# The last products of a hybrid decoder block: two pieces of 256 tokens, and final norms with tokens on partitions

## The chip, the cores and the metric

The kernel runs on one core of one Trainium2 chip. The core has TensorE (PE, matrix products into PSUM banks of 128 partitions by 512 fp32 columns), VectorE (DVE), ScalarE (ACT), GpSimd (POOL) and SyncE (SP, which issues the transfers here). The metric is the device time of one launch in microseconds, the median of several runs. The program before takes 983.76 us (three runs, 981.42 to 987.34).

## The reference

One decoder block on x of 1024 tokens by 1024 features in fp32, with shift, scale and gate columns made from a vector c:

```python
    for i in range(DEPTH):
        cond = c_act @ ada_w[i] + ada_b[i]
        shift1, scale1, gate1, shift2, scale2, gate2 = jnp.split(cond, N_MOD, axis=-1)
        h = modulate(rmsnorm(x, norm1_g[i]), shift1, scale1)
        ...
        x = x + gate1[:, None, :] * (y @ w_out[i])

        h2 = modulate(rmsnorm(x, norm2_g[i]), shift2, scale2)
        g_ff, up_ff = jnp.split(h2 @ w_ffn_in[i], 2, axis=-1)
        x = x + gate2[:, None, :] * ((jax.nn.silu(g_ff) * up_ff) @ w_ffn_out[i])

    shift_f, scale_f = jnp.split(c_act @ ada_f_w + ada_f_b, 2, axis=-1)
    return modulate(rmsnorm(x, norm_f_g), shift_f, scale_f)
```

What matters here is the end: the product with `w_ffn_out`, its addition to x, and the final norm over the 1024 features of each token, with its scale and shift.

## The kernel before

Everything is held with features on partitions: x is sixteen tiles of 128 features by 512 tokens, eight (k = 0 to 7) for each half of the tokens (half 0: tokens 0 to 511, half 1: 512 to 1023). Matmuls take fp32 operands split into a high and a low part, and three matmuls stand for one product of a 128x128 weight tile.

The feed-forward's second product is computed by a scheme of seven products in place of eight (Strassen-Winograd, on the two halves of the tokens and the two halves of features), in three rounds over the inner dimension (`ROUNDS`: 4, 4 and 3 pairs of tiles). For each n of 0 to 3 there are seven products m, each over the round's pairs; in the last round one product is 3 pairs x 3 matmuls = nine matmuls of 512 columns. `step(n, m)` (L1408) runs one: products 1, 6, 7, 4 add up in a bank B, 5 and 3 in a bank C, 2 in a bank A, and after each product DVE adds the bank's present state, times the gate, to one x tile (L1419). `DESTS` says to which: 1, 2 and 4 go to half 0, and 5, 7, 6 and 3 to half 1; 2 and 3 finish the tile k = n of their half, 4 and 5 finish k = n + 4. So half 0 is done with (3, 4), half 1 with the last of the C products. `begin_out(n)` loads and splits the weights of n; with `KEPT` those of products 5 and 3 for n = 1 to 3 lie in buffers that nothing else needs then.

In the last round the list at L1442 gives the order: behind half 0's last product (3, 4) come (1, 3), (2, 3), (3, 5) and (3, 3), of which only (3, 3) is cut into two pieces of 256 tokens. `pieces` (L1327) are half 0, and the first and second 256 tokens of half 1; each has a final norm of its own.

The final norm: `square` (L1339) squares a finished x tile on ACT (L1343). Early squares are added up on POOL (L1348) into `sums`; late ones go straight to `to_partitions` (L1330), which sums over the 128 features on PE: `ones` spread to 32 columns is the stationary side, 128 tokens of the square are the moving side, and the four groups of tokens land on four groups of 32 partitions (L1335). `early_sums` (L1354) does so for the POOL sums. `norm(i)` (L1359) takes the root on ACT (L1364), the reciprocal on DVE (L1365; both on tiles with 128 columns) and spreads the result over all partitions by matmuls (L1367) with a picking column `sel_tok` as the stationary side. `output(i)` (L1370) multiplies x with scale and norm on DVE (L1385), or on POOL (L1382) from a copy (L1376), adds the shift on ACT (L1387, L1383) and stores rows of 512 columns (L1389).

The order of each engine is not that of the text. `fix_order` (L493) takes all instructions, gives each a duration (`duration`, L131; `Clock.tensor`, L338, adds a price when PE changes between matmuls that use only part of its rows or columns and whole ones), and runs a list scheduler several times over the whole program with ranks from its own backward run; the best order found is laid down for each engine, SP's transfers with it. `issue_after` holds PE instructions behind a given one. Each engine then runs its queue in order.

Of the kernel before, what the change touches and what calls it, by code (L numbers as in the profile page):

```python
# [7 lines left out]
F32 = mybir.dt.float32  # L8
F32R = mybir.dt.float32r
BF16 = mybir.dt.bfloat16  # L10
AF = mybir.ActivationFunctionType
ALU = mybir.AluOpType
# [21 lines left out]
N_FILL = 8  # L34
N_POOL_TAPS = (6, 6)
IDLE = (0, 3, 3)
DIAGONAL = ('n2_0', 'a1', 'b1', 'n2_1', 'g10', 'g11')

SHIFT1, SCALE1, GATE1, SHIFT2, SCALE2, GATE2, SHIFTF, SCALEF = range(8)
# [91 lines left out]
def duration(s):  # L131

    width = max([o.width for o in s.reads + s.writes] or [0])
    two_in = sum(o.space == "SB" for o in s.reads) >= 2
    if s.engine == "PE":
        n, m = s.writes[0].width, s.reads[1].width
        if not s.reads[0].f32:
            t = n / 512 * 0.2267
        else:
            k = s.reads[0].box[1] - s.reads[0].box[0]  # L140
            t = {128: 0.219, 32: 0.068}.get(m, 0.109 if k > 64 else 0.055) * n / 128
        return t, t + 0.176, 0
    if s.engine == "Activation":
        psum = any(o.space == "PSUM" for o in s.reads)
        t = 0.238 + width * 0.0007 if psum else 0.2 + width * 0.00085
        t += 0.08 * sum(o.width == 1 for o in s.reads[1:])
        return (t + 0.1, t + 0.105, 0) if len(s.writes) > 1 else (t - 0.097, t + 0.009, 0)
    if s.engine == "DVE":
        if s.kind in ("Memset", "BNStatsAggregate"):
            return 0.09, 0.18, 0  # L150
        if s.kind == "BNStats":
            return 0.61, 0.7, 0
        if s.kind == "Reciprocal":
            t = 0.95 if width >= 128 else 0.17
# [174 lines left out]
class Clock:  # L329
# [7 lines left out]

    def tensor(self, t, s):  # L338

        if s.partial != self.partial:  # L340
            self.partial = s.partial
            t += 0.09 if s.partial else 0.12
        w = int(t / CLOCK_WINDOW)
        slow = 2 if self.throttled and self.active.get(w - 1, 0.0) < CLOCK_WINDOW / 2 else 1
        end = t + slow * s.issue
        a = t
        while a < end:
            w = int(a / CLOCK_WINDOW + 1e-9)
# [161 lines left out]
def block_kernel(ctx: ExitStack, tc: tile.TileContext, xT, c, ada, cols, vbias, bs, wsp,  # L510
# [88 lines left out]
    def load_late():  # L599
        t = front.tile([P, 2 * H], F32R, tag="wt", name="late")  # L600
        late.update(diag=t[:, 0:H], low=t[:, H:H + P], picks=t[:, H + P:H + P + 2 * P + 1])
        raw = tmp("picks_raw")[:, 0:2 * P + 1]
        nc.sync.dma_start(raw, cst[:, P + 34:])
        A.activation(late["picks"], raw, AF.Copy)
        G.memset(late["diag"].bitcast(F32), 0.0)

# [717 lines left out]
            nc.sync.dma_start(xs[half][i], x_mid[half][i])  # L1324


    pieces = [slice(0, H), slice(H, H + 256), slice(H + 256, S)]  # L1327
    sums, squares_in, norm_banks = {}, [0, 0, 0], {}

    def to_partitions(i, t):  # L1330

        part = pieces[i]
        nq = (part.stop - part.start) // P
        for q in range(nq):
            PE.matmul(norm_banks[i][q * 32:(q + 1) * 32, 0:P], ones.broadcast_to([P, 32]),  # L1335
                      t[:, q * P:(q + 1) * P], start=squares_in[i] == 0, stop=False, skip_group_check=True)
        squares_in[i] += 1

    def square(k, half, cols=None, late=False):  # L1339

        part = cols or (slice(0, H) if half == 0 else slice(H, S))
        t = ev(f"sq_nf{half}_{k}_{part.start}")[:, 0:part.stop - part.start]
        A.activation(t, x_tile(k, part), AF.Square)  # L1343
        if not late:
            if half not in sums:
                sums[half] = t
            else:
                G.tensor_tensor(sums[half], sums[half], t, op=ALU.add)  # L1348
            return
        for i, p in enumerate(pieces):  # L1350
            if p.start >= part.start and p.stop <= part.stop:
                to_partitions(i, t[:, p.start - part.start:p.stop - part.start])

    def early_sums(half):  # L1354
        for i, p in enumerate(pieces):
            if (p.start >= H) == (half == 1):
                to_partitions(i, sums[half][:, p.start - half * H:p.stop - half * H])

    def norm(i):  # L1359
        bank, part = norm_banks[i], pieces[i]  # L1360
        nq = (part.stop - part.start) // P
        rows = slice(0, nq * 32)
        rt = sb.tile([P, P], F32, tag="rt", name=f"rt_nf{i}", bufs=2)[rows]
        A.activation(rt, bank[rows, 0:P], AF.Sqrt, bias=epst[rows], scale=1.0 / D)  # L1364
        V.reciprocal(rt, rt)  # L1365
        for q in range(nq):
            PE.matmul(bank[:, q * P:(q + 1) * P], sel_tok[rows, q:q + 1].broadcast_to([nq * 32, P]),  # L1367
                      rt, start=True, stop=True)

    def output(i, tiles=range(KD), by_pool=()):  # L1370
        bank, part = norm_banks[i], pieces[i]
# [3 lines left out]
            r = ev(f"r_nf{i}")[:, 0:size]  # L1375
            A.activation(r, bank[:, 0:size], AF.Copy)  # L1376
        for k in tiles:
            if k % per_store == 0:
                row = ev(f"of{i}_{k}")
            t = row[:, k % per_store * size:(k % per_store + 1) * size]  # L1380
            if k in by_pool:
                G.tensor_tensor(t, x_tile(k, part), r, op=ALU.mult)  # L1382
                A.activation(t, t, AF.Identity, bias=ccol(SHIFTF, k), scale=ccol(SCALEF, k))  # L1383
            else:
                V.scalar_tensor_tensor(t, x_tile(k, part), ccol(SCALEF, k), bank[:, 0:size],  # L1385
                                       op0=ALU.mult, op1=ALU.mult)
                A.activation(t, t, AF.Identity, bias=ccol(SHIFTF, k))  # L1387
            if (k + 1) % per_store == 0:
                nc.sync.dma_start(out[(0, KD, KD + KD // 2)[i] + k // per_store], row)  # L1389
# [4 lines left out]
    for r, pairs in enumerate(ROUNDS):  # L1394
# [13 lines left out]
        def step(n, m, cols=slice(0, H)):  # L1408
# [1 line left out]
            if m == 1:  # L1410
                b_banks[n] = mm_bank(f"B{r}_{n}")
            if m == 5:
                c_banks[n] = cv_bank(f"C{r}_{n}")
            bank = c_banks[n] if m in (5, 3) else gn_bank(f"A{r}_{n}") if m == 2 else b_banks[n]
            ins = product(bank, st[n][m], [v[m] for v in mov], m in (1, 5, 2), cols)
            k, half = DESTS[m]
# [23 lines left out]
            continue  # L1440
        begin_out(0)
        for n, m in ((0, 1), (0, 5), (0, 6), (0, 2), (0, 7), (1, 1), (0, 4), (0, 3), (1, 6), (1, 2), (1, 7),  # L1442
                     (2, 1), (1, 4), (2, 2), (2, 6), (3, 1), (2, 7), (3, 2), (3, 6), (2, 4), (1, 5), (3, 7),
                     (2, 5), (3, 4)):
            if m == 1 and n:
                begin_out(n)
            last_ins = step(n, m)
            if m in (2, 4):
                if n == m == 2:
                    norm_banks[0] = nrm_bank("ssq_nf0")  # L1450
                square(n if m == 2 else n + 4, 0, late=n == 3)
            elif (n, m) in ((0, 7), (1, 5), (2, 5)):
                square(n + 4, 1)
            elif (n, m) == (0, 3):
                square(0, 1)
            if (n, m) == (3, 7):
                early_sums(0)


    with issue_after(last_ins):  # L1460
        step(1, 3)
        square(1, 1)
        norm(0)
        step(2, 3)
        norm_banks[1], norm_banks[2] = gn_bank("ssq_nf1"), mm_bank("ssq_nf2")
        square(2, 1, late=True)
        early_sums(1)
        step(3, 5)
        square(7, 1, late=True)
        output(0, (0, 1, 2, 4), by_pool=())  # L1470
        for part in pieces[1:]:
            step(3, 3, slice(part.start - H, part.stop - H))
            square(3, 1, part, late=True)
    with tc.high_priority():
        norm(1)
        norm(2)
    output(0, (3, 5, 6, 7), by_pool=(3, 5))
    output(1)
    output(2)

# [82 lines left out]
```

## Time and profile before

| | |
|---|---|
| runs | 983.76 us median (981.42, 983.76, 987.34) |
| profiled execution | 983.2 us, of which its span is 981.5 us |
| PE busy | 956.0 us, 97% of the span |
| DVE busy | 873.5 us, 89% |
| mean granted clock of TensorE | 0.994 |
| transfers | 142.18 MB read, 41.16 MB written |

The span is cut into 40 slices on the page; a digit is the busy share in tenths:

```profile
PE   7999999999999999999999999999999999999994
DVE  6989999989999762899999999999778989869936
ACT  6777467543473752564332233333337437236416
POOL 0068888656464312665444444455442200000121
PEclk9999999999999999999999999999999999999997
```

In a row of the timeline or of a group stand the engine, the line, the operation, the tile written and the tiles read, and the count; "x8" behind a line of four matmuls says that each fp32 matmul is two instructions. A matmul's duration contains its way through the array, so that the distance between starts is shorter than the duration of one. The chain of waits goes back from the program's end and names at each step what released the next. A table by stretches gives for each stretch the busy time of each engine with its count of instructions, the granted clock, the share of the transfer engines that was busy, and GB/s.

### The profile page before, as it was taken

The numbers are of one execution on the slowest core, as the hardware profiler recorded it, in microseconds if no ns is written. First come the engines' busy times: TensorE is split into PE (matmuls) and PEld (weight loads), VectorE is DVE, ScalarE is ACT, GpSimd is POOL, SyncE is SP. The second block draws the span as 40 slices with busy tenths as digits, with TensorE's granted clock in tenths as the row PEclk, the third lists the DMA queues.
The fourth block names the chain that finished last, engine by engine and source line by source line (L and its number), as shares of the span: only waits on it lengthen the run. The fifth ranks groups of instructions, "written<-read, shape, count | busy, mean of one in ns | idle before, by whom it ended". The sixth has DMA issues, their size and how long they took to land.

```text
span 981.5 us, 13035 instructions
## 1 busy us (share of the span) xinstructions
PE 956.0 (97%) x4563; PEld 769.1 (78%) x4563; DVE 873.5 (89%) x1232; ACT 475.1 (48%) x755; POOL 403.6 (41%) x233
## 2 busy tenths in 40 slices
PE   7999999999999999999999999999999999999994
PEld 4877777778777778788888878888887888888873
DVE  6989999989999762899999999999778989869936
ACT  6777467543473752564332233333337437236416
POOL 0068888656464312665444444455442200000121
PEclk9999999999999999999999999999999999999997
DMA  9982442434476434744677776867657848315104
GB/s 341 334 317 69 164 158 64 143 122 150 144 249 192 145 133 160 264 174 150 214 242 238 240 247 232 260 226 252 202 185 263 285 155 261 112 56 159 33 1 172
DMA packets 70355, 184.19 MB, mean 188 GB/s; under 512 B 7825, under 2 KB 8209, under 8 KB 70290
## 3 DMA queue, kind: packets, MB, share of 16 engines
q1 hardware_dynamic: 70290, 183.37, 55.8%
q8 instruction: 36, 0.59, 0.3%
q14 instruction: 29, 0.24, 0.1%
HBM read 142.18 MB, written 41.16 MB: 187 GB/s over the span
## 4 chain that ended last, share of the span: by engine, by line
PE 76%; DVE 17%; ACT 2%; issue 2%; DMA 2%; POOL 1%; SPq 0%; ACTq 0%; DVEq 0%; POOLq 0%
PE B L1065 27%; PE C L1065 16%; PE ah L1065 9%; DVE cv L998 6%; PE po L675 3%; PE po L677 3%; PE po L676 3%; PE p L675 3%; PE A L1065 3%; PE p L676 3%; PE p L677 3%; DVE w_f L1058 1%; DVE ada L629 1%; DVE t_h L687 1%; PE pm L939 1%
## 5 line engine op out<-in xcount | busy, mean ns | idle before, releaser
L1065 PE MATMUL B<-h,w_f 128*128 128x512 f32 x816 | 190.3, 390 | 1.3 <-DVE x L1285 0.9
L1065 PEld LDWEIGHTS B<-h,w_f 128*128 128x128 f32 x816 | 152.8, 188 | 34.7 <-DVE x L1285 1.7
L998 DVE SCALAR_TENSOR_TENSOR cv<-ypad,colt,cv 128x512 f32<-128x512 f32 x216 | 146.6, 746 | 0.1
L1065 PE MATMUL B<-fa,w_d 128*128 128x512 f32 x528 | 125.7, 390 | 0.3 <-DVE x L1419 0.3
L1065 PE MATMUL C<-h,w_f 128*128 128x512 f32 x528 | 123.4, 389 | 0.0
L1065 PEld LDWEIGHTS B<-fa,w_d 128*128 128x128 f32 x528 | 98.7, 188 | 22.0 <-DVE x L1419 0.8
L1065 PEld LDWEIGHTS C<-h,w_f 128*128 128x128 f32 x528 | 99.1, 188 | 20.6
L1065 PE MATMUL ah<-h,wh_a 128*128 128x512 f32 x320 | 101.8, 395 | 1.1 <-DVE ahead L1082 0.7
L1057 ACT ACTIVATE w_d<-raw_d 128x512 fp32r<-128x512 f32 (+1 forms) x72 | 42.1, 594 | 84.1 <-PE B L1065 33.0
L1348 POOL TENSOR_TENSOR sq_nf<-sq_nf,sq_nf 128x512 f32<-128x512 f32 x9 | 12.5, 1389 | 170.5 <-ACT sq_nf L1343 170.5
L659 POOL TENSOR_TENSOR wl_a<-raw_a,wh_a 128x1024 fp32r<-128x1024 f32 x20 | 49.6, 2481 | 78.0 <-ACT wh_a L658 78.0
L1308 POOL TENSOR_TENSOR x<-x,up 128x512 f32<-128x512 f32 x20 | 34.8, 1741 | 101.6 <-ACT x L1307 101.6
L1057 ACT ACTIVATE w_f<-raw_f 128x512 fp32r<-128x512 f32 x68 | 42.4, 627 | 67.6 <-PE B L1065 37.3
L1065 PEld LDWEIGHTS ah<-h,wh_a 128*128 128x128 f32 x320 | 59.8, 188 | 16.3 <-issue 1.2
L1058 DVE TENSOR_TENSOR w_f<-raw_f,w_f 128x512 fp32r<-128x512 f32 x68 | 70.4, 1040 | 2.4 <-ACT w_f L1057 2.2
L1065 PE MATMUL C<-fa,w_d 128*128 128x512 f32 (+1 forms) x273 | 64.4, 384 | 0.0
L1065 PE MATMUL ah<-h,wl_a 128*128 128x512 f32 x160 | 62.7, 393 | 0.0
L1065 PEld LDWEIGHTS C<-fa,w_d 128*128 128x128 f32 x273 | 50.0, 188 | 10.8 <-issue 1.0
L1058 DVE TENSOR_TENSOR fa<-a,fa 128x512 fp32r<-128x512 f32 x77 | 52.4, 721 | 1.3 <-ACT fa L1057 1.2
L1419 DVE SCALAR_TENSOR_TENSOR x<-B,cond,x 128x512 f32<-128x512 f32 x48 | 35.6, 744 | 18.8 <-PE B L1065 18.6
L1057 ACT ACTIVATE fa<-a 128x512 fp32r<-128x512 f32 x77 | 46.4, 626 | 6.0 <-DMA a<-acts 2.9
L1058 DVE TENSOR_TENSOR w_d<-raw_d,w_d 128x512 fp32r<-128x512 f32 (+1 forms) x72 | 46.8, 660 | 2.2 <-ACT w_d L1057 2.2
(268 smaller groups left out, 2118.4 us busy)
## 6 DMA issues: line engine op xcount, KB each, us to landing
acts<-x SPq DMA_DIRECT2D x77, 256.0 KB, 3.0
a<-acts SPq DMA_DIRECT2D x77, 256.0 KB, 4.3
raw_f<-wf SPq DMA_DIRECT2D x32, 512.0 KB, 4.0
ada<-ada SPq DMA_DIRECT2D x24, 512.0 KB, 3.6
x<-ada SPq DMA_DIRECT2D x24, 512.0 KB, 4.1
raw_a<-wf SPq DMA_DIRECT2D x20, 512.0 KB, 3.8
ahead<-ahead SPq DMA_DIRECT2D x40, 256.0 KB, 3.9
ypad<-ada SPq DMA_DIRECT2D x16, 512.0 KB, 6.0
```

The costliest lines, as they stand in the source:

```text
L629: V.scalar_tensor_tensor(raw, raw, 1.0, cact, op0=ALU.mult, op1=ALU.mult, accum_out=cond[:, j:j + 1])
L659: lo_eng.tensor_tensor(lo[:, cut], raw[:, cut], hi[:, cut].bitcast(F32), op=ALU.subtract)
L675: PE.matmul(acc, shi, mhi, start=start, stop=False)
L676: PE.matmul(acc, slo, mhi, start=False, stop=False)
L677: PE.matmul(acc, shi, mlo, start=False, stop=stop)
L998: V.scalar_tensor_tensor(accs[j], src, wc, accs[j], op0=ALU.mult, op1=ALU.add)
L1057: A.activation(dst[:, 0, :], src, AF.Copy)
L1058: lo_eng.tensor_tensor(dst[:, 1, :], src, dst[:, 0, :].bitcast(F32), op=ALU.subtract)
L1065: last_mm = PE.matmul(bank[:, cols], s, m[:, cols], start=first and p == 0 and i == 0, stop=p == n - 1 and i == 2, skip_group_check=True)
L1308: G.tensor_tensor(g0, g0, up0, op=ALU.mult)
L1348: G.tensor_tensor(sums[half], sums[half], t, op=ALU.add)
L1419: V.scalar_tensor_tensor(x_tile(k, part), bank[:, cols], ccol(GATE2, k), x_tile(k, part), op0=ALU.mult, op1=ALU.add)
```

## The change

In the last round's list, (1, 5) and (2, 5) are moved from before half 0's last product (3, 4) to behind it, and (3, 2) is moved to just before it. Behind (3, 4) stand six products: (1, 5), (2, 5), (3, 5) over all of half 1, and then (1, 3), (2, 3), (3, 3) for the first 256 tokens and again for the second. All squares of half 0, and those of half 1 but for (3, 3), are added on POOL; only the last goes straight to PE. The C bank of n = 3 comes from the B banks' tag.

The sums over features have the square (128 features by 128 tokens) as the stationary side and one column of ones as the moving side, so that the result has tokens on partitions, one column for 128 tokens. Root and reciprocal run on 4 or 2 columns. Spreading uses the reciprocal's column, repeated to 128 columns, as the stationary side and a unit matrix `eye`, loaded from an enlarged constant array, as the moving side. POOL takes no part in the outputs (`BY_POOL` is empty), and half 0's outputs are written to buffers of the "act0" tag, two to a buffer, each stored by itself.

The planner's prices change too: a matmul with 128 stationary columns costs at least as much as one of 128 moving columns, and going back from partial to whole matmuls costs 0.113 more.

```diff
+BEFORE_LAST = ((3, 6), (2, 4), (3, 7), (3, 2))
+AFTER_LAST = ((1, 5), (2, 5), (3, 5))
+IN_PIECES = (1, 2, 3)
+BY_POOL = ()
...
-            t = {128: 0.219, 32: 0.068}.get(m, 0.109 if k > 64 else 0.055) * n / 128
+            t = {128: 0.219, 32: 0.068}.get(m, 0.109 if k > 64 else 0.055) * (max(n, P) if m == P else n) / 128
...
+        again = 0.0
         if s.partial != self.partial:
             self.partial = s.partial
             t += 0.09 if s.partial else 0.12
+            again = 0.0 if s.partial else 0.113
...
-        end = t + slow * s.issue
+        end = t + slow * s.issue + again
...
+    eye = sb.tile([P, P], F32, tag="rt", name="eye", bufs=2)
+    nc.sync.dma_start(eye, cst[:, P + 34 + 2 * P + 1:])
...
-        nq = (part.stop - part.start) // P
-        for q in range(nq):
-            PE.matmul(norm_banks[i][q * 32:(q + 1) * 32, 0:P], ones.broadcast_to([P, 32]),
-                      t[:, q * P:(q + 1) * P], start=squares_in[i] == 0, stop=False, skip_group_check=True)
+        for q in range((part.stop - part.start) // P):
+            PE.matmul(norm_banks[i][:, q:q + 1], t[:, q * P:(q + 1) * P], ones,
+                      start=squares_in[i] == q == 0, stop=False, skip_group_check=True)
...
-                G.tensor_tensor(sums[half], sums[half], t, op=ALU.add)
+                run = sums[half][:, part.start - half * H:part.stop - half * H]
+                G.tensor_tensor(run, run, t, op=ALU.add)
...
-        rows = slice(0, nq * 32)
-        rt = sb.tile([P, P], F32, tag="rt", name=f"rt_nf{i}", bufs=2)[rows]
-        A.activation(rt, bank[rows, 0:P], AF.Sqrt, bias=epst[rows], scale=1.0 / D)
+        rt = const.tile([P, nq], F32, name=f"rt_nf{i}")
+        A.activation(rt, bank[:, 0:nq], AF.Sqrt, bias=epst, scale=1.0 / D)
         V.reciprocal(rt, rt)
         for q in range(nq):
-            PE.matmul(bank[:, q * P:(q + 1) * P], sel_tok[rows, q:q + 1].broadcast_to([nq * 32, P]),
-                      rt, start=True, stop=True)
+            PE.matmul(bank[:, q * P:(q + 1) * P], rt[:, q:q + 1].broadcast_to([P, P]), eye,
+                      start=True, stop=True)
...
-                c_banks[n] = cv_bank(f"C{r}_{n}")
+                c_banks[n] = (mm_bank if last_round and n == 3 else cv_bank)(f"C{r}_{n}")
...
-                     (2, 1), (1, 4), (2, 2), (2, 6), (3, 1), (2, 7), (3, 2), (3, 6), (2, 4), (1, 5), (3, 7),
-                     (2, 5), (3, 4)):
+                     (2, 1), (1, 4), (2, 2), (2, 6), (3, 1), (2, 7)) + BEFORE_LAST + ((3, 4),):
...
-                square(n if m == 2 else n + 4, 0, late=n == 3)
+                square(n if m == 2 else n + 4, 0)
...
-            if (n, m) == (3, 7):
-                early_sums(0)
+        early_sums(0)
...
+    def rest(n, m):
+        step(n, m)
+        square(n + 4 if m == 5 else n, 1)
...
     with issue_after(last_ins):
-        step(1, 3)
-        square(1, 1)
+        rest(*AFTER_LAST[0])
         norm(0)
-        step(2, 3)
+        for n, m in AFTER_LAST[1:]:
+            rest(n, m)
+        output(0, by_pool=BY_POOL)
         norm_banks[1], norm_banks[2] = gn_bank("ssq_nf1"), mm_bank("ssq_nf2")
-        square(2, 1, late=True)
-        early_sums(1)
-        step(3, 5)
-        square(7, 1, late=True)
-        output(0, (0, 1, 2, 4), by_pool=())
-        for part in pieces[1:]:
-            step(3, 3, slice(part.start - H, part.stop - H))
-            square(3, 1, part, late=True)
-    with tc.high_priority():
-        norm(1)
-        norm(2)
-    output(0, (3, 5, 6, 7), by_pool=(3, 5))
+        for i in (1, 2):
+            part = pieces[i]
+            cols = slice(part.start - H, part.stop - H)
+            for n in IN_PIECES:
+                step(n, 3, cols)
+                square(n, 1, part, late=n == IN_PIECES[-1])
+                if len(IN_PIECES) > 1 and n == IN_PIECES[-2]:
+                    early_sums(1, (i,))
+            if len(IN_PIECES) == 1 and i == 1:
+                early_sums(1)
+            with tc.high_priority():
+                norm(i)
     output(1)
     output(2)
```

More of the change, by code (lines that the diff above doesn't have):

```diff
@@ L602, in load_late @@
         raw = tmp("picks_raw")[:, 0:2 * P + 1]
-        nc.sync.dma_start(raw, cst[:, P + 34:])
+        nc.sync.dma_start(raw, cst[:, P + 34:P + 34 + 2 * P + 1])
         A.activation(late["picks"], raw, AF.Copy)
@@ L1352, in square, with early_sums @@
                 to_partitions(i, t[:, p.start - part.start:p.stop - part.start])
-    def early_sums(half):
+    def early_sums(half, parts=(0, 1, 2)):
         for i, p in enumerate(pieces):
-            if (p.start >= H) == (half == 1):
+            if i in parts and (p.start >= H) == (half == 1):
                 to_partitions(i, sums[half][:, p.start - half * H:p.stop - half * H])
@@ L1377, in output @@
         for k in tiles:
-            if k % per_store == 0:
+            if i == 0:
+                if k % 2 == 0:
+                    rows = sb.tile([P, 2, H], F32, tag="act0", name=f"of{i}_{k}", bufs=8)
+                row = rows[:, k % 2, :]
+            elif k % per_store == 0:
                 row = ev(f"of{i}_{k}")
@@ L1530 @@
                 low_rows=-(part[:, None] // 16 % 2), sel_hl=((part == 0) | (part == 32))[:, None])
-    cst = np.concatenate([np.eye(P) - same, gind, picks], axis=1).astype(np.float32)
+    cst = np.concatenate([np.eye(P) - same, gind, picks, np.eye(P)], axis=1).astype(np.float32)
     arrays = dict(
```

## The prediction

> **What bounds the kernel now.** First the page's top, then the table by stretches for the end of the program, cut where the last product of half 0 ends (954.02) and where the last product of all ends (966.45).
>
> ```profile
> span 981.5 us, 13035 instructions
> PE 956.0 (97%) x4563; PEld 769.1 (78%) x4563; DVE 873.5 (89%) x1232; ACT 475.1 (48%) x755; POOL 403.6 (41%) x233
> ...
> core 0: us, PE busy (x) PEld busy (x) DVE busy (x) ACT busy (x) POOL busy (x), PEclk, DMA share, GB/s
> 900.00:940.00 40.00, 40.00 (x177) 33.06 (x177) 36.56 (x60) 17.39 (x32) 7.34 (x5) 1.00 0.13 40
> ...
> 934.30:954.02 19.72, 19.72 (x99) 15.52 (x99) 6.79 (x10) 2.53 (x4) 4.21 (x4) 1.00 0.00 1
> 954.02:966.45 12.43, 12.42 (x90) 9.67 (x88) 6.98 (x10) 6.28 (x11) 2.20 (x2) 1.00 0.11 41
> 966.45:981.50 15.05, 2.27 (x12) 1.58 (x12) 9.77 (x21) 10.39 (x23) 2.49 (x2) 0.58 0.64 246
> ```
>
> PE is busy without a gap until 966.45; then come 15.05 us in which it does 2.27 us of work. So the end has two terms: when the last product finishes (I call it T, now 966.45), and what follows T. From 900 to 934 DVE is nearly full (36.56 of 40 us) making weights, yet PE never stands, and from 934.30 DVE is only a third busy: the weights are all there, so products behind that point can change places without waiting for weights.
>
> The chain of waits through the end tells the price of each piece:
>
> ```profile
> 932.46 6.12 PE B L1065 x27
> ...
> 942.44 0.36 PE ssq_nf L1335 x8
> ...
> 949.72 2.27 PE C L1065 x9
> ...
> 955.84 0.35 PE ssq_nf L1335 x8
> ...
> 960.72 0.89 PE ssq_nf L1367 x8
> 961.61 0.34 PE ssq_nf L1335 x2
> 961.95 1.26 PE C L1065 x9
> 963.21 1.43 PE ssq_nf L1335 x22
> 964.64 0.91 PE C L1065 x6
> 965.54 0.34 PE ssq_nf L1335 x4
> 965.89 0.56 PE C L1065 x3
> 966.45 0.03 issue
> 966.48 0.50 DVE x L1419
> ...
> 967.05 0.42 ACT sq_nf L1343
> ...
> 967.52 0.43 PE ssq_nf L1335 x4
> ```
>
> A whole product is nine matmuls: 6.12 / 3 = 2.04 us. A half product: (0.91 - 0.56) / 3 = 0.117 a matmul, 1.05 for nine. What is left over where products start again behind a group of sums, 2.27 - 2.04 = 0.23 and 0.91 - 6 x 0.117 = 0.21, is the price of going back from the 32-column sums to full-width matmuls: 0.22.
>
> **The change, part by part.**
>
> *Sums and norms on PE ahead of T.* Removed: three groups of eight instructions for half 0 (the first 0.36, the last 0.35), then 0.34, 1.43 and 0.34 for half 1, in all 3.2 us; six returns at 0.22, 1.3; and the norm of half 0, which is spread over the tokens by 0.89. That is 5.4. Added: the sum of a square now has the squares as the stationary side and one column moving, one matmul for 128 tokens, two instructions each as the rows' counts show. Ahead of T stand four for half 0, four for piece 1, two early ones for piece 2: ten matmuls, 20 instructions; then the spreading for half 0 (8 instructions) and piece 1 (4). No row shows a 128-column weight load with one column moving. The nearest is the spreading with full weights, 0.89 / 8 = 0.111; from below the 32-column sums, 0.36 / 8 = 0.045; from above a weight load that nothing overlaps, 0.19 (row below). I take 0.111, for it loads weights of the same shape: 32 x 0.111 = 3.56. These are full width, so no returns: 0, and at most 0.22 for each of some seven groups.
>
> *Half products.* Six halves and ten whole in place of two halves and twelve whole: 4 x 1.05 - 2 x 2.04 = +0.12. Each half uses its bank again only two half products later, so the wait for DVE's read is covered by 2 x 1.05 against 0.53; without the cover it would be about 0.5 a time.
>
> T is then 966.45 - 5.4 + 3.56 + 0.12 = 964.7.
>
> *Behind T.* The rows for it: first groups of equal shape (the 256-wide ones from the stretch behind 966.45, the others from 954.02 to 966.45, L909 and L910 from the whole program), then the timeline, last the end of the chain:
>
> ```profile
> L1385 DVE SCALAR_TENSOR_TENSOR of<-x,cond,ssq_nf 128x256 f32<-128x256 f32 x16 | 6.3, 468 | 0.0
> L1387 ACT ACTIVATE of<-of,cond 128x256 f32<-128x256 f32 x16 | 6.5, 492 | 0.0
> ...
> L1385 DVE SCALAR_TENSOR_TENSOR of<-x,cond,ssq_nf 128x512 f32<-128x512 f32 x4 | 2.8, 743 | 0.1
> L1343 ACT ACTIVATE sq_nf<-x 128x512 f32<-128x512 f32 x4 | 2.5, 634 | 5.1 <-DVE x L1419 3.7 <-POOL sq_nf L1348 1.4
> L1419 DVE SCALAR_TENSOR_TENSOR x<-C,cond,x 128x512 f32<-128x512 f32 x3 | 2.3, 751 | 3.6 <-PE C L1065 3.6
> L1367 PEld LDWEIGHTS ssq_nf<-rt_nf,sel_tok 128*128 128x128 f32 x8 | 1.0, 190 | 0.1
> ...
> L909 ACT ACTIVATE sd<-mv,epst 128x4 f32<-128x4 f32 x2 | 0.6, 298 | 1.2 <-DVE mv L905 1.2
> L910 DVE RECIPROCAL sd<-sd 128x4 f32<-128x4 f32 x2 | 0.3, 166 | 0.0
> L1365 DVE RECIPROCAL rt_nf<-rt_nf 64x128 f32<-64x128 f32 x2 | 1.9, 938 | 0.6 <-ACT rt_nf L1364 0.6
> ...
> 967.86 0.71 PE L1367 MATMUL ssq_nf<-rt_nf,sel_tok 64*128 64x128 f32 x4
> ...
> 958.28 1.29 POOL L1348 TENSOR_TENSOR sq_nf<-sq_nf,sq_nf 128x512 f32<-128x512 f32 x1 [3.34 <-ACT sq_nf L1343]
> 969.25 7.57 DVE L1385 SCALAR_TENSOR_TENSOR of<-x,cond,ssq_nf 128x512 f32<-128x512 f32 x18
> 969.38 1.22 PE L1367 MATMUL ssq_nf<-rt_nf,sel_tok 64*128 64x128 f32 x4 [0.80 <-DVE rt_nf L1365]
> ...
> 977.66 0.80 ACT of L1387 x2
> ```
>
> Now, eighteen output operations stand on DVE behind 969.25 (7.57 us), with ACT behind them to 978.46, and the store's landing and the end take 981.5 - 978.46 = 3.04. In the new kernel only the eight of the last piece have to come behind T. The chain: add and square of the last half product as now, 967.52 - 966.45 = 1.07. Ahead of the last sum stands the early sum of that piece, which waits for POOL: the half product before it ended 1.05 earlier, so it is T - 1.05 + 1.03 + POOL's add. That add is 256 wide, between half of 1.29 and all of it; 0.7 and 0.1 for signals give T + 0.8, and four instructions 0.44, so the last sum starts at T + 1.24 and not at T + 1.07. Its four instructions with the way out: 3 x 0.111 + 0.27 = 0.6. Root on two columns 0.30 (the 128x4 row), reciprocal 0.17 (same; it was 0.94 on 128 columns), signals 0.1, spreading 0.6 to 0.71 as in the row at 967.86: DVE can start at T + 3.0. Then eight at 6.3 / 16 = 0.39, ACT one behind at 6.5 / 16 = 0.41: the last ACT ends 0.47 + 7 x 0.41 + 0.49 = 3.8 later, T + 6.8; with 3.04, T + 9.85 = 974.55.
>
> Two additions. The spreading ran 1.22 for four instructions at 969.38 where 0.71 was usual: PE's granted clock is 0.58 in the mean of the last 15.05 us, which with halves means full speed for 2.4 us behind T. The new spreading falls at T + 2.4, on that edge: I add half of 0.5, 0.25. The Trainium skill, page "TensorE: Matmul & The Clock Gate", section "Why this matters for your kernels", warns of idle gaps of more than about 3 us between bursts; by it the spreading here, with sums less than 1 us before, would run at full speed and the sum be 0.25 lower. This trace disagrees: the clock fell with no gap of PE longer than 1.1 us.
>
> The other is DVE's queue. Half 0's norm now goes through one more POOL add (1.29): behind its last product add 0.78, square 0.70, POOL 1.36, sum 0.95, root and reciprocal 0.55, spreading 0.95, in all 5.3. That product ends 3 x 2.04 + 6 x 1.05 + 3.56 = 16.0 ahead of T, so half 0's output can start 10.7 ahead of T. Until piece 2's norm, at T + 3.0, DVE has 13.7 us and owes two whole adds (1.5), six half adds (2.9), eight outputs at 2.8 / 4 = 0.70 (5.6), eight at 0.39 (3.1) and two reciprocals (0.3): 13.4. It just fits, because POOL's two outputs and the 0.94 reciprocals are gone or smaller. Since DVE runs in order, an add or reciprocal on the path can wait behind one output (0.70) or two: I add 0.5, of 0 to 1.4. ACT's share of the same stretch is less. The stores of half 0 (eight, as before) leave while the DMA share is near zero (0.11 in the row to 966.45), so they cost nothing; without that cover they would stand ahead of the last store.
>
> The load of the unit matrix is one transfer of 64 KB in a stretch with a DMA share of 0.00 to 0.13; nothing waits on SP behind it for long: 0. The third bank of C for n = 3 comes from the pool of the B banks, where a finished one is free: 0, bounded by one product's add (0.75) if not.
>
> Sum: 974.55 + 0.25 + 0.5 = 975.3 for the span. The profiled run has 983.2 for 981.5, so 1.7 more lie around it, and it is 0.6 under the median of 983.76. **Forecast: 977.0 us.** A difference counts from 0.5%, 4.9 us: below 978.8 is faster, above 988.7 slower.
>
> **The rivals.**
>
> *The output of half 0 is not hidden.* DVE's 13.4 of 13.7 us leave nothing over; if the order puts half 0's norm or outputs late, they stand behind T. All 24 outputs behind T + 0.5 are 5.6 + 6.3 = 11.9, then 0.9 of ACT and 3.04: 964.7 + 16.3 + 1.7 = 982.7. For: DVE full by count. Against: the norm is ready 10.7 us ahead of T, and up to T DVE has nothing more urgent than adds of 0.5 to 0.75. No change.
>
> *Weight loads of the sums don't overlap.* At 0.19 in place of 0.111, twenty instructions ahead of T and eight behind give 28 x 0.079 = 2.2: 979.2, within 0.5%. For: a single column moves while 128 columns load. Against: the spreading's loads last 190 each and still follow at 0.111.
>
> *The plan is made anew.* The order of every engine comes from a planner, and the change raises its price of a return to full width by 0.113 in the whole program. The small matmuls lie mostly between 20 and 400:
>
> ```profile
> 20.00:100.00 80.00, 78.56 (x401) 63.58 (x400) 76.97 (x107) 60.71 (x92) 37.59 (x24) 1.00 0.68 240
> 100.00:200.00 100.00, 99.55 (x594) 77.72 (x594) 98.97 (x143) 60.04 (x92) 81.74 (x42) 1.00 0.42 137
> 200.00:300.00 100.00, 98.25 (x466) 77.82 (x465) 96.59 (x147) 52.13 (x73) 54.45 (x27) 1.00 0.51 168
> 300.00:400.00 100.00, 97.85 (x478) 76.81 (x476) 67.68 (x97) 47.12 (x67) 29.46 (x15) 1.00 0.48 161
> ```
>
> PE stands 1.44 + 0.45 + 1.75 + 2.15 = 5.8 us there, and DVE is at 97 to 99% up to 300: what a new order makes late on DVE, PE waits for. If it triples PE's idle time, 11.6 more, the result is 988.6; it decides from 6.8 more, where the gain is gone, and with 12 it is slower: 989. For: DVE has no slack. Against: the higher price is nearer to the rows (0.22 measured, 0.12 before in the plan), and PE is near full whichever order serves it.
>
> *All goes well.* No backlog on DVE, sums nearer to 0.045, clock kept: 977.0 - 0.5 - 0.25 - 20 x 0.066 = 974.9.
>
> **How the numbers follow.** Forecast (975.5 to 978.8) 0.58; half 0 not hidden 0.12; loads not overlapped 0.10, of which I count half as faster; new plan 0.10; all well 0.10. Faster: 0.58 + 0.10 + 0.05 = 0.73; same 0.12 + 0.05 = 0.17; slower 0.10. The range from 974.0 to 983.0 takes in all but the slower plan, and the bounds of each term.
>
> **What would show it.** T at 964.7 within 1 us and PE without gaps to there; sums at about 0.111 an instruction and no 0.22 behind them; eight DVE outputs of width 256 behind piece 2's spreading, and last product to end about 10.5 us in place of 15.05; reciprocals near 0.17. It is wrong if outputs of half 0 stand behind T, if sums take 0.19, if PE's idle time between 20 and 934 grows by more than 2 us.

## The result, and the profile after

The changed kernel takes 971.28 us (median of four runs, 969.98 to 972.04), the kernel before 982.59 us on the same chip (981.21 to 987.34): a ratio of 0.9875 with a 95% interval of 0.9838 to 0.9912. That is 11.3 us faster; the forecast was 977.0, and the range ended at 974.0. The direction held; the forecast gain of 6.8 us (983.76 to 977.0) was three fifths of it.

The profiled execution took 971.88 us. The top of its page:

```profile
span 970.1 us, 13012 instructions
PE 951.9 (98%) x4549; PEld 770.1 (79%) x4549; DVE 878.1 (91%) x1236; ACT 475.3 (49%) x756; POOL 401.9 (41%) x237
```

PE's busy time fell by 4.1 us and the span by 11.4, so 7.3 us are time in which PE stood. To see where, both traces are cut at two places that every variant here has: the first matmul with the bias of v (some 118 us from the start) and the first matmul into a bank A of the last stage (some 755 us). The table by stretches of the kernel before, the middle and then the end (columns: stretch, its length, PE, PEld, DVE, ACT and POOL busy, clock, DMA share, GB/s):

```profile
117.95:756.05 638.10, 632.43 (x3018) 510.27 (x3016) 582.19 (x776) 291.56 (x451) 328.98 (x183) 1.00 0.59 194
756.05:981.50 225.45, 212.40 (x982) 173.43 (x980) 184.85 (x296) 103.38 (x184) 20.62 (x14) 0.97 0.42 139
```

The same two stretches of the kernel after:

```profile
118.30:751.16 632.86, 630.70 (x3017) 510.43 (x3016) 587.97 (x781) 293.47 (x454) 327.71 (x183) 1.00 0.59 196
751.16:970.10 218.94, 209.97 (x968) 174.62 (x966) 183.73 (x299) 100.81 (x182) 21.01 (x18) 0.99 0.43 141
```

The end, which is all that the edit of the program touches, is 6.5 us shorter (225.45 to 218.94). The middle, whose instructions are the same ones, is 5.2 us shorter too. PE stood there for 638.10 - 632.43 = 5.67 us before and for 632.86 - 630.70 = 2.16 us after. The start, up to the first cut, was 0.35 us longer (117.95 to 118.30). So the forecast's own terms gave in sum about what they promised, and the rest came from a part of the program for which its sum had no term.

The chain of waits of the kernel after, behind half 0's last product (which ends at 943.84):

```profile
943.84 3.17 PE C L1071 x14
947.01 0.83 PE ssq_nf L1343 x8
947.84 1.04 PE C L1071 x4
948.87 0.89 PE ssq_nf L1375 x8
949.76 7.58 PE C L1071 x55
957.35 0.79 PE ssq_nf L1343 x8
958.14 1.07 PE C L1071 x8
...
959.23 0.47 DVE x L1431
...
960.26 1.31 ACT of L1399 x3
961.57 0.15 ACT rt_nf L1372
961.71 2.73 ACT of L1399 x7
...
964.49 2.10 ACT of L1399 x5
966.59 0.40 ACTq L1571
```

Sums with the squares as the stationary side take 0.83 / 8 = 0.10 us an instruction. The last product ends at 959.21, and 10.89 us follow it, against 15.05 before. The timeline of PE behind that point:

```profile
959.03 0.60 PE L1375 MATMUL ssq_nf<-eye,rt_nf 128*128 128x128 f32 x4
959.66 1.16 PE L1343 MATMUL ssq_nf<-ones,sq_nf 128*128 128x1 f32 x8
962.31 0.71 PE L1375 MATMUL ssq_nf<-eye,rt_nf 128*128 128x128 f32 x4 [1.49 <-DVE rt_nf L1373]
```

Between the last sum (done by 960.82) and the last spreading (962.31) lie 1.49 us, of which the timelines of ACT and DVE show the work itself to be short and the queues to be full:

```profile
961.47 0.24 ACT L1372 ACTIVATE rt_nf<-ssq_nf,epst 128x2 f32<-128x2 f32 x1
961.62 5.38 ACT L1399 ACTIVATE of<-of,cond 128x256 f32<-128x256 f32 x13
962.10 0.16 DVE L1373 RECIPROCAL rt_nf<-rt_nf 128x2 f32<-128x2 f32 x1
962.17 4.18 DVE L1397 SCALAR_TENSOR_TENSOR of<-x,cond,ssq_nf 128x256 f32<-128x256 f32 x10
```

The root starts 0.65 us behind the last sum (ACT is in piece 1's outputs), and the reciprocal 0.39 behind the root (DVE is in them too). All sixteen outputs of 256 columns, those of both pieces, run behind the last product, since piece 1's norm is spread only at 959.03. The chain shows what they cost: from 960.26 to 966.59 it is ACT, which does fifteen of them and the root with no gap above 0.04 us, and not the sums, reciprocal and spreading of piece 2.

### The profile page after: what moved, and what is told of

The parts are those of the page before. It is cut to its first block, busy times and chain, and to the rows that moved or that the text cites. A ratio compares the mean times of both kernels' runs of the same rounds, so it can differ in the third digit from the quotient of the medians.

```text
span 970.1 us, 13012 instructions
## 1 busy us (share of the span) xinstructions
PE 951.9 (98%) x4549; PEld 770.1 (79%) x4549; DVE 878.1 (91%) x1236; ACT 475.3 (49%) x756; POOL 401.9 (41%) x237
## 4 chain that ended last, share of the span: by engine, by line
PE 75%; DVE 19%; ACT 3%; issue 2%; DMA 2%; SPq 0%; ACTq 0%; DVEq 0%
PE B L1071 29%; PE C L1071 18%; PE ah L1071 9%; DVE cv L1004 6%; PE A L1071 3%; PE v L681 2%; PE v L683 2%; PE v L682 2%; PE po L681 2%; PE po L682 1%; PE po L683 1%; DVE ypad L635 1%; DVE ada L635 1%; DMA ada<-ada 1%; DVE w_f L1064 1%
## 5 line engine op out<-in xcount | busy, mean ns | idle before, releaser
L1357 POOL TENSOR_TENSOR sq_nf<-sq_nf,sq_nf 128x512 f32<-128x512 f32 (+1 forms) x15 | 18.1, 1204 | 177.5 <-ACT sq_nf L1351 177.3
```

Source lines behind the costliest of these rows:

```text
L1357: G.tensor_tensor(run, run, t, op=ALU.add)
```

## The experiments

All medians stand beside runs of the kernel before on the same chip, which gave 982.73 to 983.18 us. The stretches are cut as above. First the four kernels that separate the planner's price from the program's end: neither, one, the other, both. Before and after are two of them.

**The end alone.** The kernel after with the price of a return at zero. The other new price, that of matmuls with 128 stationary columns, stays:

```diff
-            again = 0.0 if s.partial else 0.113
+            again = 0.0
```

> The kernel after without the planner's new price for a return to full width (0.113 set to 0); the program and its tail are unchanged, and the order of PE is then that of the kernel before up to the last round. Theory A (the 5 us that the forecast missed come from the order that the new price gives between 0 and 750 us): the first matmul of the last-but-two stage (A<-fa) is back at 756, as before, T comes near 964, and the time is 976 to 977. Rival B (the gain beyond the tail comes from the changed end of the program, whose ranks run back through everything): 971 to 972, as after. Rival C (the early part differs from run to run): the early milestones scatter and have nothing to do with the order.

976.23 us (975.87 to 979.42), ratio 0.9930 with an interval of 0.9905 to 0.9954. Its stretches:

```profile
117.57:755.18 637.61, 631.95 (x3018) 510.45 (x3016) 581.47 (x776) 291.58 (x451) 329.98 (x183) 1.00 0.59 194
755.18:974.16 218.98, 210.37 (x968) 175.15 (x966) 183.46 (x300) 102.89 (x185) 22.79 (x18) 0.98 0.43 144
```

The middle is that of before (637.61 against 638.10, PE standing 5.66 us), the end that of after. The rows of PE in the two traces have the same order up to 938 us, and those of DVE up to 909, so the price that stayed moves nothing ahead of the end. This is the kernel that the forecast had in mind, and 977.0 is 0.8 from it.

**The prices alone.** The kernel before with the two new prices in `duration` and `Clock.tensor`, and nothing else:

```diff
-            t = {128: 0.219, 32: 0.068}.get(m, 0.109 if k > 64 else 0.055) * n / 128
+            t = {128: 0.219, 32: 0.068}.get(m, 0.109 if k > 64 else 0.055) * (max(n, P) if m == P else n) / 128
...
+        again = 0.0
         if s.partial != self.partial:
             self.partial = s.partial
             t += 0.09 if s.partial else 0.12
+            again = 0.0 if s.partial else 0.113
...
-        end = t + slow * s.issue
+        end = t + slow * s.issue + again
```

> The kernel before with the two new planner prices and nothing else; program and tail are those of before, the order of the first stages that of after. Theory A: the stages up to 753 are 4.9 us earlier, the tail is still 15 us behind T, and the time is 977 to 979. Rival B: 982 to 984, as before. Rival C: as for the run without the price, no system in it.

977.04 us (976.11 to 977.92), ratio 0.9933 (0.9910 to 0.9957):

```profile
116.33:749.75 633.42, 630.92 (x3017) 510.44 (x3016) 586.65 (x781) 293.68 (x454) 326.75 (x183) 1.00 0.60 196
749.75:974.66 224.91, 211.61 (x982) 173.04 (x980) 184.53 (x295) 100.67 (x181) 17.67 (x14) 0.98 0.42 137
```

Now the middle is that of after and the end that of before. Theory A holds in both runs, and the rivals fall: the price alone moves the middle by some 5 us, the program's end alone moves the end by 6.5, and in the stretches the two nearly add up (6.5 and 4.7, against 11.7 with both). (The medians alone would not show it so well: they fell by 7.0 and 6.1 us, together 1.8 more than the 11.3.)

What the price did there is seen where PE waited. The longest waits of PE in the middle of the kernel before:

```profile
PE po L675 <- ACT y_b L956: 1.6, 1, 1.6
PE B L1065 <- DVE x L1285: 0.9, 2, 0.5
PE ah L1065 <- DVE ahead L1082: 0.7, 1, 0.7
```

and of the kernel after (in us: in total, times, longest):

```profile
PE po L681 <- ACT y_b L962: 0.7, 1, 0.7
PE B L1071 <- DVE x L1291: 0.4, 1, 0.4
PE gn L1024 <- ACT y_a L962: 0.3, 1, 0.3
PE ah L1071 <- ACT h L698: 0.3, 1, 0.3
```

The waits are at much the same places and shorter. No stage was removed; the same instructions stand in another order. Whether PE comes later to its inputs or they are ready sooner was not measured.

**Is the price right, or was the order lucky?** If the gain comes from a price nearer to the chip, it should follow the price. Four kernels are the kernel after with another number in place of 0.113: 0.06, 0.10, 0.13, 0.20.

> The kernel after with a return price of 0.06 in the planner in place of 0.113; program unchanged. Theory D (the gain comes because the price is nearer to what the chip does): between the run without the price (976.2) and after (971.3), 973 to 975, stretch from the v-bias matmuls to the first A<-fa some 635. Rival E (any new price deals the order anew, and this one was a lucky draw): anywhere from 970 to 978, no order in the prices.

> As above with 0.10. Theory D: 971 to 972, as after, stretch 633. Rival E: anywhere from 970 to 978.

> As above with 0.13. Theory D: 971 to 972, stretch 633. Rival E: anywhere from 970 to 978.

> As above with 0.20, which makes a return cost 0.32 in all, above the 0.22 that the rows show. Theory D: worse than after again, 973 to 975. Rival E: anywhere from 970 to 978.

| price | median us (range) | ratio, 95% interval | middle us | PE standing in it | end us |
|---|---|---|---|---|---|
| 0 | 976.23 (975.87 to 979.42) | 0.9930 (0.9905 to 0.9954) | 637.61 | 5.66 | 218.98 |
| 0.06 | 971.39 (969.16 to 972.73) | 0.9883 (0.9860 to 0.9905) | 632.56 | 1.73 | 218.66 |
| 0.10 | 973.53 (973.07 to 974.27) | 0.9909 (0.9888 to 0.9931) | 634.77 | 1.94 | 218.63 |
| 0.113 | 971.28 (969.98 to 972.04) | 0.9875 (0.9838 to 0.9912) | 632.86 | 2.16 | 218.94 |
| 0.13 | 977.83 (975.66 to 983.80) | 0.9956 (0.9939 to 0.9972) | 640.93 | 7.39 | 218.62 |
| 0.20 | 978.73 (976.45 to 978.97) | 0.9954 (0.9938 to 0.9971) | 640.01 | 6.19 | 218.79 |

The end is the same within 0.4 us in all six, and the whole difference lies in the middle. Between 0.113 and 0.13, both near enough to the 0.22 in all that the rows show (the plan already had 0.12 of it), the middle moves by 8 us; 0.06 is as good as 0.113. Theory D's order does not appear: none of the four medians lies in the range that it gave. Only in one point does it fit, that the two extremes, no price and 0.20, are not among the good ones. (0.20 is also 0.7 above the range of rival E.) The middle of the run with 0.13, and PE's longest waits in it:

```profile
116.04:756.97 640.93, 633.54 (x3017) 510.82 (x3016) 583.07 (x773) 291.49 (x452) 329.78 (x183) 1.00 0.58 193
```

```profile
PE ah L1071 <- ACT h L698: 2.8, 1, 2.8
PE B L1071 <- ACT x L1289: 1.4, 1, 1.4
```

Here PE waited for 2.8 us in one piece for ACT in front of the first products of the feed-forward, which the kernel after shows for 0.3 us. The wait cost more than itself. Right behind it, from 272.78 to 276.19, the granted clock (the third number from the right) was half:

```profile
272.78:276.19 3.41, 3.30 (x8) 2.02 (x7) 3.41 (x7) 3.41 (x7) 0.00 (x0) 0.50 1.01 351
```

Matmuls of 512 columns followed each other there at some 0.43 us in place of 0.227, by which about 1.6 of the 3.41 us were lost (an estimate from these two distances). Wait and clock together are some 4 of the 8.1 us between this middle and that of the kernel after. The run with 0.20 has one such stretch too (355.37 to 358.78); the kernels before and after have none in the middle.

The returns themselves hardly count. The middle of the kernel before has 22 returns ahead of whole products, that of after 19; at 0.22 each that is 0.7 of the 5.2 us. And the run with 0.06 has 22, as before, and a middle 5.5 us shorter all the same.

**A trifle in the planner.** To see whether any perturbation deals the order anew, DVE's signal time in the planner is raised by 2 ns, in the kernel after and in the kernel before:

```diff
-SIGNAL = {"PE": 0.043, "DVE": 0.024, "Activation": 0.024, "Pool": 0.068, "SP": 0.05}
+SIGNAL = {"PE": 0.043, "DVE": 0.026, "Activation": 0.024, "Pool": 0.068, "SP": 0.05}
```

> The kernel after, with DVE's signal time in the planner 0.026 in place of 0.024 us and nothing else; the order of PE is the same for the first 753 of 2548 rows, then differs in places. Rival E (the order is a draw): the stretch from the v-bias matmuls to the first A<-fa leaves the 632.4 to 633.4 that four runs of nearly one order gave, by 1 us or more, either way. Theory D' (the order is stable against such a trifle and only the return price deals it anew): within 632 to 634, time 970.5 to 972.5.

> The kernel before with the same 2 ns and no other edit; PE's order is the same for 1100 of 2546 rows. Rival E: the stretch leaves 637.6 to 638.1 by 1 us or more, and a gain or loss appears without any change of the program. Theory D': 637 to 639, time 982 to 984.

After with 2 ns: 971.86 us (971.24 to 972.97), ratio 0.9885 (0.9865 to 0.9904), and the middle is 634.91, outside the 632.4 to 633.4 of the runs with the order of after, by 1.5. Before with 2 ns: 982.11 us (981.43 to 983.05), ratio 0.9992 (0.9982 to 1.0001), the middle 637.13, within 1 us of before. So a trifle moved the middle by 2.1 us in the one case and by 1.0 in the other, where profiled executions of one order differ by up to 1.0 among themselves, and a new price moved it by up to 8. Rival E is borne out for the prices and, for trifles, in one of two cases.

**The old form of sums and norms.** The kernel after with ones over 32 columns as the stationary side, root and reciprocal on 128 columns:

```diff
-    eye = sb.tile([P, P], F32, tag="rt", name="eye", bufs=2)
-    nc.sync.dma_start(eye, cst[:, P + 34 + 2 * P + 1:])
...
-        for q in range((part.stop - part.start) // P):
-            PE.matmul(norm_banks[i][:, q:q + 1], t[:, q * P:(q + 1) * P], ones,
-                      start=squares_in[i] == q == 0, stop=False, skip_group_check=True)
+        nq = (part.stop - part.start) // P
+        for q in range(nq):
+            PE.matmul(norm_banks[i][q * 32:(q + 1) * 32, 0:P], ones.broadcast_to([P, 32]),
+                      t[:, q * P:(q + 1) * P], start=squares_in[i] == 0, stop=False, skip_group_check=True)
...
-        rt = const.tile([P, nq], F32, name=f"rt_nf{i}")
-        A.activation(rt, bank[:, 0:nq], AF.Sqrt, bias=epst, scale=1.0 / D)
+        rows = slice(0, nq * 32)
+        rt = sb.tile([P, P], F32, tag="rt", name=f"rt_nf{i}", bufs=2)[rows]
+        A.activation(rt, bank[rows, 0:P], AF.Sqrt, bias=epst[rows], scale=1.0 / D)
...
-            PE.matmul(bank[:, q * P:(q + 1) * P], rt[:, q:q + 1].broadcast_to([P, P]), eye,
-                      start=True, stop=True)
+            PE.matmul(bank[:, q * P:(q + 1) * P], sel_tok[rows, q:q + 1].broadcast_to([nq * 32, P]),
+                      rt, start=True, stop=True)
```

> The kernel after with sums and norms in the old form (ones as the stationary side over 32 columns, tokens along the free side, root and reciprocal on 128 columns, spreading by the picking column; no unit matrix). Theory (columns save mainly the reciprocal on the path behind T, 0.94 against 0.17, and the root 0.36 against 0.25): the part behind T is 0.9 longer, T moves by less than 0.3 since shorter sums and returns of 0.22 nearly cancel; 972.5 to 973. Rival (full weight loads for one column cost more than they save): 970.5 to 971.3, T earlier by 1.

The median is 971.45 us (971.01 to 971.64), ratio 0.9875 (0.9850 to 0.9900), no different from after and in neither of the two ranges. The stretches tell more:

```profile
116.38:749.40 633.02, 630.76 (x3017) 510.45 (x3016) 586.37 (x781) 294.50 (x454) 327.33 (x183) 1.00 0.59 196
749.40:969.29 219.89, 209.73 (x968) 173.25 (x966) 185.43 (x299) 101.58 (x182) 20.77 (x18) 0.98 0.42 141
```

Two rows of PE's timeline at its end, the last half products and the last spreading:

```profile
955.76 1.21 PE L1071 MATMUL C<-fa,w_d 128*128 128x256 f32 x8
...
961.07 1.22 PE L1375 MATMUL ssq_nf<-rt_nf,sel_tok 64*128 64x128 f32 x4 [2.23 <-DVE rt_nf L1373]
```

The end is 0.95 us longer than after's. The last product ended at 956.97, 207.57 behind the stretch's start (after: 959.21 - 751.16 = 208.05), and 12.32 followed it (after: 10.89). Of these 1.43 us, 0.53 is the clock and not the form of the norms: the last spreading ran for 1.22 us here and for 0.71 in the kernel after, and the run without the price, which has the new form and 1.22 as well, has 974.16 - 962.74 = 11.42 us behind its last product. The other 0.90 is the old form, which is the size that the theory gave; PE's longer wait for the reciprocal (2.23 against 1.49) shows most of it. Against that run the last product did not move either (962.74 - 755.18 = 207.56). That the profiled execution is nevertheless no longer than after's is due to its start: it reached 749.40 earlier because its first 118 us were 1.9 us shorter (116.38 against 118.30) with the same order of PE there, which the order of the end can't have done. One us in a single median of such runs is not resolved.

**One product in pieces, not three.** (1, 3) and (2, 3) whole, in front of (3, 3) in two pieces:

```diff
-AFTER_LAST = ((1, 5), (2, 5), (3, 5))
-IN_PIECES = (1, 2, 3)
+AFTER_LAST = ((1, 5), (2, 5), (3, 5), (1, 3), (2, 3))
+IN_PIECES = (3,)
```

> The kernel after with only the last product (3, 3) in two pieces; (1, 3) and (2, 3) run whole before it. Theory (three products in pieces put piece 1's norm and output under piece 2's products): piece 1's norm is ready some 2 us later against T, 16 outputs stand nearly whole behind T, the part behind T grows by 1 to 2, and the time is 972.5 to 973.5. Rival (output 1 is not on the path): within 0.4 of after.

972.42 us (971.02 to 974.54), ratio 0.9890 (0.9861 to 0.9920); the end is 220.25 us, 1.3 more than after's, and the part behind the last product (969.31 - 956.84 = 12.47, with the last spreading at full clock) is 1.6 longer, in the theory's range of 1 to 2. What cutting three products adds to the gain is thus 1.3 us in this pair of profiles; the median is just below the range that the theory gave, and the medians' intervals overlap.

PE's timeline has the wait that half products of other banks had covered, the second half product waiting for DVE's read of the first from the same bank:

```profile
955.04 0.98 PE L1071 MATMUL C<-fa,w_d 128*128 128x256 f32 x6 [0.58 <-DVE x L1431]
```

**Two of half 0's outputs on POOL.** `BY_POOL = (3, 5)` in the kernel after.

> The kernel after with two of half 0's eight outputs multiplied on POOL (BY_POOL = (3, 5)); the order of the first 2518 rows of PE is unchanged. If DVE's queue of 13.4 us in 13.7 is what the end hangs on, 2 x 0.7 less on DVE brings the part from the first A<-fa to the end down by 0.5 to 1. Rival (ACT and the last piece's own outputs set the end, half 0's outputs are hidden anyway): within 0.3; or longer by 0.5 to 1 where POOL's outputs of 1.27 each stand in front of its adds of squares.

971.27 us (970.43 to 972.99), ratio 0.9881 (0.9861 to 0.9902); the end is 219.54, longer by 0.6. DVE got its room and stood in it, and the last spreading of PE was slow:

```profile
957.73 2.44 DVE L1397 SCALAR_TENSOR_TENSOR of<-x,cond,ssq_nf 128x256 f32<-128x256 f32 x6 [0.87 <-PE ssq_nf L1375]
...
960.30 1.22 PE L1375 MATMUL ssq_nf<-eye,rt_nf 128*128 128x128 f32 x4 [1.14 <-DVE rt_nf L1373]
961.63 3.22 DVE L1397 SCALAR_TENSOR_TENSOR of<-x,cond,ssq_nf 128x256 f32<-128x256 f32 x8 [0.62 <-PE ssq_nf L1375]
```

DVE waited 0.87 and 0.62 us for the norms of the pieces, so relief on its count of 13.4 in 13.7 us bought nothing here. The run is no clean test of that count, though. The planner also put piece 1's sums behind the last product, which the kernel after has ahead of it, and the last spreading ran for 1.22 us in place of 0.71. And DVE still stood in the way in one place: piece 2's reciprocal started 0.63 us behind its root, in the midst of piece 1's outputs. What the kernel after would gain from a DVE with less to do stays open; its own chain ends on ACT.

## Why the prediction was wrong in size

**The step that failed** is a term of the sum that was put at nothing: the time ahead of the last round. The sum moves T and what follows it and takes the first 756 us as unchanged. The rival "The plan is made anew" named the place (20 to 400, where PE stood 5.8 us) and the cause (a new price in the planner, which orders the whole program), and then charged it only as a loss; the range's lower end of 974.0 gave the order no gain at all. The two-by-two of prices and program shows that term to be -5.2 us in the profiled pair: 3.5 of it are standing time in the middle, from 5.67 to 2.16 us, and 1.7 PE's busy time. The other prices show that it could have been +3 us as well (640.93 against 638.10). A range that took the 5.8 us of standing time as what a new order might win would have reached to about 971.

**The terms of the end** held in sum. The forecast took 981.5 - 975.3 = 6.2 us off the span; the end is 6.5 shorter, in the run with the order of before 6.5 too (225.45 to 218.98). The path was in part another one, so that some of the closeness is luck.

- *T.* From the first matmul into A the last product ended 210.40 us on before and 208.05 after, 2.35 earlier where 1.75 was forecast. The sums cost 0.10 an instruction, near the 0.111 taken and far from 0.19, so "weight loads don't overlap" fell. Piece 1's spreading and piece 2's early sums came behind T and not ahead of it, 24 instructions in place of 32. Returns were not nothing: whole products behind a group took 0.13 more than their count (1.04 - 4 x 0.227), inside the bound of 0.22.
- *Behind T.* 10.89 us where 975.3 - 964.7 = 10.6 was forecast. The forecast's path was sums, root, reciprocal, spreading and then the eight outputs of piece 2, with ACT's share called less than DVE's. In the trace all sixteen narrow outputs run behind T, and the chain ends on ACT, which is in them without a break. The two paths are nearly as long as each other: in the run without the price, where the spreading took 0.5 longer, the chain goes through reciprocal and spreading and the part behind T is 0.53 longer. The queues' share was taken as 0.5 and put on DVE; on the way to the spreading it was 0.65 on ACT and 0.39 on DVE. Root and reciprocal on two columns took 0.24 and 0.16, near the 0.30 and 0.17 of the small rows.
- *Clock.* Half of 0.5 was added for a spreading on the clock's edge. In the profiles it is one or the other: 0.71 in the kernel after, 1.22 in the run without the price (the rows are below). With 1.22 the part behind T is 11.4 us (two runs with this end), with 0.71 to 0.77 it is 10.9 to 11.0 (five), so the 0.5 was the right price of the bad case.
- *The output of half 0 hidden* held: its eight outputs ended at 958.14, ahead of T, so that rival fell. By the median of 2.0 us from issue to landing the last of its stores lands some 1 us behind T, and the transfer engines are nearly idle behind it (a share of 0.05 from 960 to 961), so nothing waits for it. "DVE's queue just fits" was a true count; whether it is also a bound isn't settled by the run with POOL.
- *Half products*: the 0.12 us charged for them is too little to be told apart within T, and the wait they cover is the 0.58 us of the run with one product in pieces.

**What stays open:** why one order suits the chip better than another with nearly the same prices. The waits name late operands (h, y_b, x), yet no run here moved one of them alone. In the run with 0.13 a wait and the half clock behind it make up about half of the difference from the kernel after; the rest is spread over smaller ones.

## What to carry to other kernels

Where a program's order comes from a planner, an edit of a price is an edit of the whole program: read the trace at milestones far from the edit, and separate price and program in a two-by-two before crediting either. Give a re-plan a term with both signs; the standing time of the engine that bounds the stage is a first measure of what it can win. Before crediting a small difference at a program's end to an edit, compare executions with the same granted clock there: in three of these runs half a microsecond behind the last product was the clock. And a price that is nearer to the measured cost isn't thereby a better plan: here 0.113 gave 971.3 and 0.13 gave 977.8, so several plans are worth measuring.

## What the runs showed of the hardware that was not expected

**The clock falls on a grid of 3.413 us.** Two executions with nearly the same end differ in their last spreading. Of the run without the price, the timeline of PE:

```profile
963.20 1.16 PE L1343 MATMUL ssq_nf<-ones,sq_nf 128*128 128x1 f32 x8
965.85 1.22 PE L1375 MATMUL ssq_nf<-eye,rt_nf 128*128 128x128 f32 x4 [1.49 <-DVE rt_nf L1373]
```

The gap of 1.49 us is the same as in the kernel after, where the four instructions took 0.71. The difference is when the granted clock fell to half. In the run without the price that was at 965.76, just ahead of the spreading:

```profile
962.35:965.76 3.41, 1.98 (x16) 1.67 (x14) 2.97 (x9) 2.39 (x7) 0.73 (x1) 1.00 0.27 104
965.76:974.10 8.34, 1.22 (x4) 0.93 (x4) 4.02 (x11) 4.82 (x12) 0.00 (x0) 0.50 0.64 242
```

In the kernel after it was at 964.26, behind the spreading, which had ended at 963.02:

```profile
964.26:970.10 5.84, 0.00 (x0) 0.00 (x0) 2.09 (x6) 2.73 (x7) 0.00 (x0) 0.50 0.64 239
```

The traces' record of the granted clock holds only the values 1.0 and 0.5. It begins with full clock 14.3 to 17.5 us behind the start of the span, and in all thirteen profiled executions every stretch of full clock lasted a whole number of times 3.413 us: 277 to 279 times up to the fall at the end (278 times, 948.91 us, in both executions above), 75 and 203 times around the half clock in the middle of the run with 0.13, 99 and 179 times in the run with 0.20. The stretch of half clock in each of these two middles lasted 3.41 us, one step. At the end the fall came 2.3 to 5.7 us behind the last product. The last spreading ran for 1.22 us in the five executions in which the fall came ahead of it, and at full speed in seven in which it came later; in the run with 0.20 the fall came in its midst, and it took 0.77.

The Trainium skill, page "TensorE: Matmul & The Clock Gate", section "What's actually happening", describes a window of about 3.4 us that runs freely and isn't reset by the kernel. The traces agree: the steps are 3.413 us long, and their place against the program's start differs by up to 3.2 us from one execution to the next. What makes the clock fall at one step and not at another is not worked out here: the kernel before stood for 1.57 us within one step (from 355.11) and kept its clock, and the run with 0.20 lost it right behind the same wait (353.76 to 355.33).

**A weight load for a single column.** An fp32 weight load of 128 columns for a single moving column ran at 0.10 us an instruction, about as fast as the load for 128 moving columns (0.11).

**The start scatters.** The first 118 us of the program took 116.15 to 118.30 us in the five profiled executions whose order of PE and DVE is that of the kernel after up to 900 us. That is as much as several of the effects measured here.
